# Four instead of three of eight k pairs in the 7-product form, in the three double gate groups of a hybrid attention block

## The chip, the cores and the metric

The kernel runs on one core of a Trainium2 chip. A core has TensorE (PE: matrix products into PSUM), VectorE (DVE: elementwise work on two tensors), ScalarE (ACT: copies, casts and functions), GpSimd (POOL) and SyncE (SP), which issues most DMAs. Each engine works through its own queue in order and waits on semaphores for the others. The metric is the device time of one execution in microseconds (us), as the median of several runs; the kernel before takes 1462.29 us.

## The reference: what is computed

One layer of a residual block over 256 tokens of width 2048, in fp32:

```python
h    = rmsnorm(x, g_mix)
proj = h @ w_in                       # 2048 x 10240: q,k,v | q,k,v | gate_sb | gate_ca
y_sb = stick_breaking_attention(q_sb, k_sb, v_sb)      # 8 heads of 128
y_ca = chunked_relpos_attention(q_ca, k_ca, v_ca, rel_bias)
merged = sigmoid(gate_sb) * (y_sb @ w_sb_out) + sigmoid(gate_ca) * (y_ca @ w_ca_out)
x = x + merged @ w_mix_out
g_ff, u_ff = split(rmsnorm(x, g_ffn) @ w_ffn_in)
x = x + (silu(g_ff) * u_ff) @ w_ffn_out
x = x + sigmoid(rmsnorm(x, g_ple) @ w_ple_gate) * (p @ w_ple_in)
out = rmsnorm(x, g_final)
```

The change lies in the product that gives the two gates, gate_sb and gate_ca: h (256 x 2048) by 2048 x 2048 each.

## The kernel before, in words

**Precision.** Every operand is held as a high part (a cast to fp32r) and a low part (what the cast left). A product of a weight tile with an activation tile is three matmuls: high by high, high by low, low by high (`three`, lines 274 to 277). Weights are streamed from HBM as fp32 tiles of 128 x 1024 (two k tiles of 128 by 512 columns) called `raw`, 512 KB each; ScalarE casts the high part `hi` (line 246, `split`), VectorE subtracts to get the low part `lo` (`minus`, line 228).

**Plain pairs.** The contraction over 2048 runs over 16 k tiles, taken as eight pairs (0 to 7). A double group (`unit`, lines 164 to 183) makes two column blocks of 512 at once, for both token tiles of 128. Per k pair this is a 2 x 2 by 2 x 2 block product: eight products of three matmuls, 24 matmuls. A plain pair comes as two halves, one for each column block, with one `raw`, one `hi` and one `lo` each, and 12 matmuls each.

**Pairs in the 7-product form.** Pairs 2, 4 and 6 (`PAIRS`) are made as seven products of sums and differences, in the manner of Strassen and Winograd: 21 matmuls. For that, `split_pair` (lines 251 to 271) takes both column blocks at once. VectorE makes four differences 512 wide (three into the tile `xf`, one in place in `raw`); ScalarE casts the two raw tiles (lines 261 and 264) and then `xf` (1536 wide, line 267); VectorE makes the three low parts. The 1536-wide parts go into `room`, one place for all pairs of a group, so it is written again only when the pair before has been multiplied. The activations' sums are made ahead in a table, one form per pair: `pair_sums` (line 808 and following) with VectorE and one cast of ScalarE, through a work tile. The forms of the gate groups are in `F_gate`: two in the tile `FP`, one at the end of `room`.

**Sums.** Four of the seven products go to PSUM sums of their own (`su`), kept over all pairs of a group; three go straight into the sums of the plain products (`mm`). After a group's last pair, `mid` (line 817 and following) copies the first sum (ScalarE, line 821) and adds the others (VectorE, line 823, four adds). After the last plain pair `add_sums` (line 827) adds the plain sums, two adds per column block.

**The stage.** The gates' first 512 columns are two ordinary row groups. Then come three double groups, c = 1, 2, 3, each over both gates' columns c, from about 361 us to 486 us of the profile. The last attention steps of the chunked mixer run between these groups as `tasks`; `flush(4)` lets one task go every fourth piece, and the first pair of a double group lets all remaining ones go (`pair_products`, line 288). The value tiles (`v`, tag "v", two places in the pool `mid`) hold the values of attention; the `work` tile takes the place of the last but one of them.

**What sets the order.** `flush` walks through the list of pieces: `prefetch` loads raw tiles while at most five are held, and splits up to three pieces ahead, as long as the pieces from the current one on need at most four `hi`/`lo` buffers; then the piece's products are issued. From this program order a scheduler with its own timeline puts each engine's instructions into a fixed order before the run: where an engine would stand idle it takes a later one that is ready.

The pieces of a double group, "-" for a pair in the 7-product form: 0, 0, 1, 1, -2, 3, 3, -4, 5, 5, -6, 7, 7. The code around the change:

Of the kernel before, what the change touches and what calls it, by code (L numbers as in the profile page):

```python
# [10 lines left out]
F32R = mybir.dt.float32r  # L11
# [5 lines left out]
P = 128  # L17
S = 256
NT = 2
D = 2048  # L20
KD = D // P
HEADS = 8
W = HEADS * P
# [8 lines left out]
NB = 512  # L32
# [2 lines left out]

PAIRS = (2, 4, 6)
MIX_PAIRS = (4, 6)
RAW = 5
MORE = 2
X_LOADS = (3, 5, 6, 7)  # L40
# [3 lines left out]
def block_kernel(ctx: ExitStack, tc: tile.TileContext, x, p, w_in, w_sb_out, w_ca_out, w_mix_out,  # L44
# [43 lines left out]
    T1 = bp.tile([P, KD, 2, S], F32R, tag="T1", name="T1")  # L88
# [51 lines left out]
    pieces = []  # L140
    tasks = deque()
# [19 lines left out]
                needs=[k for k in (needs(kt) for kt in part) if k is not None],  # L161
            ))

    def unit(wsrc, n0s, kts, lhs, forms, ext, slots, mid, post, needs, row0=0, pairs=PAIRS, alone=False, after=None):


        if not alone:
            state["unit"] = state.get("unit", -1) + 1
        pool = 0 if alone else state["unit"] % 2
        g = dict(kind="unit", post=post, mid=mid, slots=slots, after=after, lhs=lhs, keep=None, forms=forms, ext=ext, pool=pool,  # L170
                 side=None if alone else 1 - pool)
        kts = list(kts)
        taken = [j for j in pairs if j < len(kts) // 2 - 1]
        for i in range(len(kts) // 2):
            part = kts[2 * i : 2 * i + 2]
            r = (row0 + 2 * i) * P
            src = [wsrc[r : r + 2 * P, n0 : n0 + NB].rearrange("(k p) n -> p k n", p=P) for n0 in n0s]
            pc = dict(g=g, kts=part, ncol=NB, needs=[needs(kt) for kt in part])
            if i in taken:
                pieces.append(dict(pc, src=src, pair=True, first=i == taken[0], last=i == taken[-1]))  # L180
            else:
                for b in range(2):
                    pieces.append(dict(pc, src=[src[b]], block=b, first=i == 0, last=2 * i + 2 == len(kts)))

    def load_x(c):
        cs = slice(c * NB, (c + 1) * NB)
# [2 lines left out]
    def load_piece(src, ncol):  # L189
        state["ring"] += 1  # L190
        if state["more"] is not None and state["ring"] % (RAW + MORE) in (0, RAW // 2 + 1):
            raw = state["more"]()
        else:
            raw = wp.tile([P, 1024], F32, tag="raw", name="raw", bufs=RAW)
        n = src.shape[1] * ncol
        return raw[:, :n], raw[:, :n].rearrange("p (k n) -> p k n", n=ncol)

    def load(pc):
        at = state["loaded"]
        pc["raw"] = []  # L200
        for src in pc["src"]:
            raw, dst = load_piece(src, pc["ncol"])
            pc["raw"].append(raw)
            state["raw"] += 1
            if at == 0:
                for k in range(2):
                    dma_w.dma_start(dst[:, k, :], src[:, k, :])
                continue
            if at in X_LOADS:
                with tc.issue_after(state["load"].ins):  # L210
                    load_x(X_LOADS.index(at))
            state["load"] = dma_w.dma_start(dst, src)
# [154 lines left out]
    def prefetch():  # L367
        while state["loaded"] < len(pieces) and state["raw"] + len(pieces[state["loaded"]]["src"]) <= RAW + (MORE if state["more"] is not None else 0):
            load(pieces[state["loaded"]])
            state["loaded"] += 1  # L370
        room = 2 if state["at"] < 4 + KD // 2 else 4 if state["fourth"] is not None else 3
        while state["split"] < state["loaded"] and state["split"] <= state["at"] + 3:
            pc = pieces[state["split"]]
            if state["split"] > state["at"] and sum(map(size, pieces[state["at"] : state["split"] + 1])) > room:
                break
            behind = [started["p"]]
            if pc["g"] is pieces[4]["g"]:
                behind += started.get(pc["kts"][0] - 2, [])
            with ExitStack() as order:
                for i in behind:  # L380
                    order.enter_context(tc.issue_after(i.ins))
                split(pc)
            state["split"] += 1

    def later(fn, n=3):

        for _ in range(n):
            tasks.append((None, lambda: None))
        tasks.append((None, fn))
# [76 lines left out]
    mp = mid_stack.enter_context(tc.tile_pool(name="mid", bufs=2))  # L466
# [75 lines left out]
    w2 = w_in[0]  # L542
    hneed = lambda kt: ("hmix", kt)

    def v_tile():
        return mp.tile([P, NT, NB], F32, tag="v", name="v")
# [55 lines left out]
    ext = ap.tile([P, HEADS, 384], F32, tag="gates", name="ext", bufs=1)  # L602
# [162 lines left out]
    def scale_table(T, kts):  # L765

        ks = slice(kts[0], kts[-1] + 1)
        by = p2bc.unsqueeze(1).to_broadcast((P, len(kts), S))
        for c in range(2):
            v = T[:, ks, c, :]  # L770
            nc.vector.tensor_tensor(v, v.bitcast(F32), by, ALU.mult)

    for mixer, make in ((0, sb_tasks), (1, ca_tasks)):
        for b in range(2):
# [3 lines left out]
            first = mixer == 0 and b == 0  # L778
            v = v0 if first else v_tile()
# [9 lines left out]
            if end:  # L789
                group("row", w2, c0 + 2 * W, range(KD), T1, lambda ps, v=v: scale_v(v, ps), needs=hneed,  # L790
                      after=lambda kts: scale_table(T1, kts))
# [9 lines left out]
    room = bp.tile([P, 4096], F32R, tag="x", name="room")  # L801
# [4 lines left out]
    F_gate = [FP[:, 0], FP[:, 1], room[:, 3072:].rearrange("p (c f s) -> p c f s", c=2, f=4)]  # L806

    def pair_sums(T, kt, f):
        af = state["work"]("af").rearrange("p (k s) -> p k s", k=2)
        hi, lo = (T.bitcast(F32)[:, kt : kt + 2, c, :] for c in range(2))  # L810
        nc.vector.tensor_tensor(af, hi, lo, ALU.add)
        sums_of(af, f)

    def gate_slots(c):
        return [gates[:, t, m, c * NB : (c + 1) * NB] for m in range(2) for t in range(NT)]
# [13 lines left out]
    for m in range(2):  # L829
        group("row", w2, 6 * W + m * D, range(KD), T1, gate_post(m, 0), needs=hneed)  # L830
    flush(3)
    for i, pair in enumerate(PAIRS):
        pair_sums(T1, 2 * pair, F_gate[i])
    for c in range(1, 4):
        unit(w2, [6 * W + m * D + c * NB for m in range(2)], range(KD), T1, lambda kt: F_gate[kt // 4 - 1],
             [room[:, :3072]], lambda c=c: gate_slots(c), mid, add_sums, hneed, alone=True)
    flush(4)
    state["fourth"] = None
    x_ = bp.tile([P, NT, D], F32, tag="x", name="x")
# [3 lines left out]
    def out_post(m, c):  # L843
        def post(ps):
# [6 lines left out]
            if m == 1:  # L851
                mg = gates[:, :, 0, cs]
                nc.vector.tensor_tensor(mg, mg, gt, ALU.add)
                later(lambda: into_table(T1, c, mg, key="mg", forms=lambda kt: FP[:, kt // 4 - 2], pairs=MIX_PAIRS))
        return post

    for c in range(4):
        for m, wo in ((0, w_sb_out), (1, w_ca_out)):
            group("row", wo[0], c * NB, range(8 * m, 8 * m + 8), T2, out_post(m, c),
                  needs=lambda kt: ("y", kt))  # L860
# [60 lines left out]
    for c in (0, 2):  # L921
        unit(w_mix_out[0], (c * NB, (c + 1) * NB), range(KD), T1, lambda kt: FP[:, kt // 4 - 2], mix_rooms, C_slots,
             mid, mix_post(c), lambda kt: ("mg", kt), pairs=MIX_PAIRS)
    flush(until=("mg", KD - 1))
# [73 lines left out]
    for blk, nk in enumerate(FF_BLOCKS):  # L998
        key = f"h{blk}"
        for c in range(nk // 4):  # L1000
            j = k0 // 4 + c
            unit(w_ffn_in[0], (j * NB, D_FF + j * NB), range(KD), T3, lambda kt: late["F"][0][kt // 4 - 1], rooms(T1),
                 C_slots, mid, (in_post if j else first_post)(T2, c, key), lambda kt: ("ffn", kt),
                 pairs=PAIRS if j else (), after=None if j else scale_next)
        last = blk == len(FF_BLOCKS) - 1
# [122 lines left out]
```

## Time and profile before

| what | value |
|---|---|
| median of 3 runs | 1462.29 us (1461.79 to 1462.46) |
| the profiled execution's own time (its span) | 1460.0 us |
| instructions | 18637 |
| bytes moved by DMA | 291.19 MB, mean 199 GB/s |
| granted TensorE clock, mean | 0.999 |

In the page, a row of the groups reads: line of the kernel, engine, operation, output tile <- input tiles, shapes, count; then the busy time in us, the mean of one in ns, and the idle time of the engine just before such instructions with what ended it. In a timeline a row is: start in us, duration, engine, line, operation, tiles, shapes, count, and in brackets the engine's idle time just before and who ended it. Durations of neighbouring instructions overlap, since they are pipelined: what one more of them costs is read from start to start. In a table of stretches each engine has its busy time in us and its count of instructions; PEld is TensorE's weight load. The idle time of an engine that is not the bottleneck costs nothing.

### The profile page before, as it was taken

What the parts mean: (1) busy time and instruction counts of PE and PEld (TensorE: products, weight loads), DVE (VectorE), ACT (ScalarE), POOL (GpSimd) and SP (SyncE); (2) the same over time, 40 slices, a digit from 0 to 9 for tenths busy, and PEclk for the clock granted to TensorE, in tenths of its full rate; (3) what the DMA queues carried; (4) which work ended last, traced back from release to release, by engine and by line L of the source; (5) the groups of instructions that cost most, each with busy time, mean ns of one, the idle gap of its engine ahead of it and who ended that gap; (6) DMA issues with size and microseconds to landing.
All of it is one profiled execution on the core that took longest, in us unless ns stands there. A gap on an engine that the chain in (4) does not pass through costs nothing.

```text
span 1460.0 us, 18637 instructions
## 1 busy us (share of the span) xinstructions
PE 1449.5 (99%) x6867; PEld 1213.5 (83%) x6867; DVE 1209.2 (83%) x1524; ACT 800.4 (55%) x950; POOL 21.9 (1%) x44
## 2 busy tenths in 40 slices
PE   9999999999999999999999999999999999999997
PEld 7888888888888888888888888888888888888886
DVE  6666667796888667988999999999999989989775
ACT  6455555557555444555555555565645555556552
POOL 0100000000000000000000000000000000000000
PEclk9999999999999999999999999999999999999999
DMA  9855555565666766766666666666666666666772
GB/s 320 283 176 174 173 173 180 179 190 161 212 196 207 236 188 188 238 191 180 194 189 200 189 208 208 202 195 210 194 195 202 203 193 195 216 199 209 229 228 73
DMA packets 164733, 291.19 MB, mean 199 GB/s; under 512 B 9025, under 2 KB 42097, under 8 KB 164385
## 3 DMA queue, kind: packets, MB, share of 16 engines
q1 hardware_dynamic: 162528, 281.32, 61.9%
q0 software_dynamic: 2112, 8.68, 1.8%
q8 instruction: 54, 0.88, 0.2%
q14 instruction: 39, 0.31, 0.1%
HBM read 284.19 MB, written 5.77 MB: 199 GB/s over the span
## 4 chain that ended last, share of the span: by engine, by line
PE 99%; DMA 0%; DVE 0%; ACT 0%; SPq 0%; issue 0%; DVEq 0%
PE mm L276 24%; PE mm L277 24%; PE mm L275 24%; PE mm L351 8%; PE mm L353 4%; PE su L275 4%; PE su L276 4%; PE su L277 4%; PE tp L434 1%; DMA raw<-in_w_ple_in 0%; PE yp L659 0%; PE xps L488 0%; PE wt L750 0%; PE mml L277 0%; PE mml L276 0%; PE mml L275 0%
## 5 line engine op out<-in xcount | busy, mean ns | idle before, releaser
L228 DVE TENSOR_TENSOR lo<-raw,hi 128x1024 fp32r<-128x1024 f32 (+1 forms) x517 | 627.5, 1220 | 168.4 <-ACT hi L246 158.6
L246 ACT CAST hi<-raw 128x1024 fp32r<-128x1024 f32 (+1 forms) x399 | 418.1, 1051 | 427.9 <-PE mm L277 316.2
L276 PE MATMUL mm<-lo,T 128*128 128x512 f32 x1391 | 542.4, 390 | 0.0
L277 PE MATMUL mm<-hi,T 128*128 128x512 f32 x1391 | 538.9, 390 | 0.0
L275 PE MATMUL mm<-hi,T 128*128 128x512 f32 x1391 | 512.6, 391 | 0.0
L277 PEld LDWEIGHTS mm<-hi,T 128*128 128x128 f32 x1391 | 261.1, 188 | 53.8
L276 PEld LDWEIGHTS mm<-lo,T 128*128 128x128 f32 x1391 | 261.2, 188 | 53.4
L275 PEld LDWEIGHTS mm<-hi,T 128*128 128x128 f32 x1391 | 260.9, 188 | 53.6
L351 PE MATMUL mm<-T,hi 128*128 128x512 f32 x512 | 180.7, 399 | 0.0
L353 PE MATMUL mm<-T,lo 128*128 128x256 f32 x512 | 140.8, 280 | 0.0
L351 PEld LDWEIGHTS mm<-T,hi 128*128 128x128 f32 x512 | 95.4, 188 | 21.5
L264 ACT CAST hi<-raw 128x1024 fp32r<-128x1024 f32 x59 | 62.3, 1055 | 70.5 <-DVE raw L228 20.0
L353 PEld LDWEIGHTS mm<-T,lo 128*128 128x128 f32 x512 | 96.4, 189 | 1.2
L228 DVE TENSOR_TENSOR T<-xf,T 128x1536 fp32r<-128x1536 f32 x50 | 87.8, 1755 | 7.9 <-ACT T L267 7.9
L228 DVE TENSOR_TENSOR xf<-raw 128x512 f32<-128x512 f32 x118 | 80.9, 686 | 9.5 <-DMA raw<-in_w_in 4.9
L267 ACT CAST T<-xf 128x1536 fp32r<-128x1536 f32 x50 | 74.0, 1480 | 7.9 <-DVE xf L228 7.8
L261 ACT CAST hi<-raw 128x1024 fp32r<-128x1024 f32 x59 | 62.2, 1054 | 28.9 <-PE mm L277 22.8
L823 DVE TENSOR_TENSOR C<-su,C 128x512 f32<-128x512 f32 x72 | 47.7, 684 | 0.2
L827 DVE TENSOR_TENSOR C<-mm,C 128x512 f32<-128x512 f32 x72 | 46.9, 683 | 0.0
L228 DVE TENSOR_TENSOR xf<-raw,xf 128x512 f32<-128x512 f32 x59 | 40.4, 685 | 0.3
L228 DVE TENSOR_TENSOR raw<-raw 128x512 f32<-128x512 f32 x59 | 40.4, 685 | 0.1
L277 PE MATMUL mm<-T,T 128*128 128x512 f32 (+1 forms) x82 | 30.2, 368 | 0.0
(310 smaller groups left out, 1369.1 us busy)
## 6 DMA issues: line engine op xcount, KB each, us to landing
raw<-in_w_ffn_in SPq DMA_DIRECT2D x176, 512.0 KB, 3.9
raw<-in_w_in SPq DMA_DIRECT2D x160, 512.0 KB, 3.6
raw<-in_w_ffn_out SPq DMA_DIRECT2D x88, 512.0 KB, 4.6
raw<-in_w_mix_out SPq DMA_DIRECT2D x32, 512.0 KB, 4.7
raw<-in_w_ple_gate SPq DMA_DIRECT2D x32, 512.0 KB, 4.8
raw<-in_w_sb_out SPq DMA_DIRECT2D x16, 512.0 KB, 4.6
raw<-in_w_ca_out SPq DMA_DIRECT2D x16, 512.0 KB, 4.6
x<-in_x SPq DMA_DIRECT2D x4, 512.0 KB, 10.3
```

Source lines behind the costliest of these rows:

```text
L228: return nc.vector.tensor_tensor(out, a, b, ALU.subtract)
L246: state["cast"] = nc.scalar.copy(hi[:, c : c + m], raw[:, c : c + m])
L261: nc.scalar.copy(h1, raw1)
L264: nc.scalar.copy(h2, raw2)
L267: nc.scalar.copy(xh, xf)
L275: nc.tensor.matmul(ps, xh, hi, start=a, stop=False)
L276: nc.tensor.matmul(ps, xh, lo, start=False, stop=False)
L277: state["mm"] = nc.tensor.matmul(ps, xl, hi, start=False, stop=z)
L351: nc.tensor.matmul(ps, hi[:, i, f], lhs[:, kt, :, :].rearrange("p c s -> p (c s)"), start=a, stop=False)
L353: nc.tensor.matmul(ps[:, :S], lo[:, i, f], lhs[:, kt, 0, :], start=False, stop=z)
L823: nc.vector.tensor_tensor(C[i], q, C[j], ALU.add)
L827: nc.vector.tensor_tensor(g["C"][i], g["ps"][i], g["C"][i], ALU.add)
```

## The change

The three double gate groups take pairs 1, 3, 5 and 6 in the 7-product form instead of 2, 4 and 6. The pieces of a group come in an order written out by hand; between pairs 1 and 3, and between 5 and 6, stands one half of a plain pair, between 3 and 5 stand two halves of different pairs:

0, 0, -1, 2, -3, 2, 4, -5, 4, -6, 7, 7

`unit` takes this list as `order`; a pair's first mention is its first column block, the second its second. Without a list it builds the same order as before, so that the other double groups (mix and feed-forward) keep theirs. Three forms are made where the three were made, for the new pairs. The fourth is made in a task that comes last in the list of tasks, in a tile that takes a place of the value tiles (tag "v"), which is free once attention has used the last values.

```diff
+GATE_PAIRS = (1, 3, 5, 6)
+GATE_ORDER = (0, 0, -1, 2, -3, 2, 4, -5, 4, -6, 7, 7)
...
-    def unit(wsrc, n0s, kts, lhs, forms, ext, slots, mid, post, needs, row0=0, pairs=PAIRS, alone=False, after=None):
+    def unit(wsrc, n0s, kts, lhs, forms, ext, slots, mid, post, needs, row0=0, pairs=PAIRS, alone=False, after=None,
+             order=None):
...
-        taken = [j for j in pairs if j < len(kts) // 2 - 1]
-        for i in range(len(kts) // 2):
+        if order is None:
+            order = [j for i in range(len(kts) // 2) for j in ([-i] if i in pairs and i < len(kts) // 2 - 1 else [i, i])]
+        taken = [-i for i in order if i < 0]
+        begun = set()
+        for i in order:
+            own = i < 0
+            i = abs(i)
...
-            if i in taken:
+            if own:
                 pieces.append(dict(pc, src=src, pair=True, first=i == taken[0], last=i == taken[-1]))
             else:
-                for b in range(2):
-                    pieces.append(dict(pc, src=[src[b]], block=b, first=i == 0, last=2 * i + 2 == len(kts)))
+                b = int(i in begun)
+                begun.add(i)
+                pieces.append(dict(pc, src=[src[b]], block=b, first=i == 0, last=2 * i + 2 == len(kts)))
...
-    for i, pair in enumerate(PAIRS):
+    for i, pair in enumerate(GATE_PAIRS[:3]):
         pair_sums(T1, 2 * pair, F_gate[i])
+
+    def last_form():
+        F_gate.append(mp.tile([P, 2, 4, P], F32R, tag="v", name="F_v"))
+        pair_sums(T1, 2 * GATE_PAIRS[3], F_gate[3])
+
+    tasks.append((None, last_form))
     for c in range(1, 4):
-        unit(w2, [6 * W + m * D + c * NB for m in range(2)], range(KD), T1, lambda kt: F_gate[kt // 4 - 1],
-             [room[:, :3072]], lambda c=c: gate_slots(c), mid, add_sums, hneed, alone=True)
+        unit(w2, [6 * W + m * D + c * NB for m in range(2)], range(KD), T1, lambda kt: F_gate[GATE_PAIRS.index(kt // 2)],
+             [room[:, :3072]], lambda c=c: gate_slots(c), mid, add_sums, hneed, alone=True, order=GATE_ORDER)
```

## The prediction

> **What bounds the kernel now.** I read the page first (busy shares and groups), then the stretch table for the three double groups, then the timelines of VectorE, ScalarE and TensorE inside the third of them.
>
> ```profile
> span 1460.0 us, 18637 instructions
> PE 1449.5 (99%) x6867; PEld 1213.5 (83%) x6867; DVE 1209.2 (83%) x1524; ACT 800.4 (55%) x950; POOL 21.9 (1%) x44
> L276 PE MATMUL mm<-lo,T 128*128 128x512 f32 x1391 | 542.4, 390 | 0.0
> ```
>
> TensorE is never released late: the last column of its groups, idle time, is 0.0. A busy 99% alone would not prove this, because matmuls overlap; their starts do.
>
> ```profile
> 463.53 0.39 PE L275 MATMUL su<-hi,T 128*128 128x512 f32 x1
> 463.75 0.39 PE L276 MATMUL su<-lo,T 128*128 128x512 f32 x1
> 463.98 0.39 PE L277 MATMUL su<-hi,T 128*128 128x512 f32 x1
> 466.25 0.39 PE L275 MATMUL su<-room,FP 128*128 128x512 f32 x1
> 466.93 0.39 PE L276 MATMUL su<-room,FP 128*128 128x512 f32 x1
> ```
>
> One matmul takes 0.39 us, but the next starts 0.22 or 0.23 us later. So a matmul that is saved is worth its step, not its 390 ns. The step comes from one period of the double groups. The copy of the first sum (line 821) marks it:
>
> ```profile
> 393.69 0.59 ACT L821 COPY gates<-su 128x512 f32<-128x512 f32 x1 [0.30 <-PE su L277]
> 435.17 0.59 ACT L821 COPY gates<-su 128x512 f32<-128x512 f32 x1 [0.26 <-PE su L277]
> 476.64 0.59 ACT L821 COPY gates<-su 128x512 f32<-128x512 f32 x1 [0.26 <-PE su L277]
> ```
>
> ```profile
> core 0: us, PE busy (x) PEld busy (x) DVE busy (x) ACT busy (x) POOL busy (x), PEclk, DMA share, GB/s
> 393.69:435.17 41.48, 41.48 (x184) 34.35 (x183) 36.04 (x40) 24.05 (x25) 0.00 (x0) 1.00 0.66 202
> 435.17:476.64 41.47, 41.47 (x184) 34.35 (x183) 36.08 (x40) 23.96 (x24) 0.00 (x0) 1.00 0.65 202
> ```
>
> A group has three pairs of 21 matmuls and five plain pairs of 24, together 183, as the weight loads (x183) show. 41.47 / 183 = 0.2266 us a step, at a granted clock of 1.00. TensorE bounds this stage. VectorE is next: 36.08 us busy, so 5.39 us idle in a group. ScalarE has 17.5 us idle, and the DMA engines work 0.65 of the time.
>
> **What the change takes away.** A fourth pair in each of three groups goes from 24 matmuls to 21: 3 x 3 x 0.2266 = 2.04 us. A group becomes 180 x 0.2266 = 40.79 us. This is all it can bring, since nothing else on TensorE goes.
>
> **What it adds on VectorE and ScalarE.** The pair form needs four 512-wide differences and a 1536-wide low part on VectorE, and a 1536-wide cast on ScalarE. The two 1024-wide casts and low parts are there in both forms. This is the last pair of the third group now:
>
> ```profile
> 464.62 0.68 DVE L228 TENSOR_TENSOR xf<-raw 128x512 f32<-128x512 f32 x1
> 465.22 1.22 DVE L228 TENSOR_TENSOR lo<-raw,hi 128x1024 fp32r<-128x1024 f32 x1
> 466.36 0.68 DVE L228 TENSOR_TENSOR raw<-raw 128x512 f32<-128x512 f32 x1
> 466.96 1.22 DVE L228 TENSOR_TENSOR lo<-raw,hi 128x1024 fp32r<-128x1024 f32 x1
> 468.09 0.68 DVE L228 TENSOR_TENSOR xf<-raw 128x512 f32<-128x512 f32 x1
> 468.70 1.22 DVE L228 TENSOR_TENSOR lo<-raw,hi 128x1024 fp32r<-128x1024 f32 x1
> 469.83 0.68 DVE L228 TENSOR_TENSOR xf<-raw,xf 128x512 f32<-128x512 f32 x1
> 472.14 1.76 DVE L228 TENSOR_TENSOR room<-xf,room 128x1536 fp32r<-128x1536 f32 x1 [1.62 <-ACT room L267]
> 473.81 3.83 DVE L228 TENSOR_TENSOR lo<-raw,hi 128x1024 fp32r<-128x1024 f32 x3
> ```
>
> Start to start a difference takes 0.60 us, a 1024-wide low part 1.13, the 1536-wide one 1.67. The new pair adds 4 x 0.60 + 1.67 = 4.07 us, and VectorE's work becomes 36.08 + 4.07 = 40.15 us in a group of 40.79. Its idle time has to shrink from 5.39 to 0.64 us, or it becomes the bound. ScalarE's extra cast (1.48 us, row below) fits into its 17.5 us.
>
> **The fourth form (last_form).** It is made once, from three kinds of rows like these:
>
> ```profile
> 324.87 0.69 DVE L811 TENSOR_TENSOR work<-T 128x512 f32<-128x512 f32 x1
> 328.46 0.28 DVE L418 TENSOR_TENSOR work<-work 128x128 f32<-128x128 f32 x1
> 328.66 0.49 DVE L228 TENSOR_TENSOR work<-work 128x128 f32<-128x128 f32 x2
> 333.12 0.69 DVE L228 TENSOR_TENSOR room<-work,room 128x512 fp32r<-128x512 f32 x1
> ```
>
> ```profile
> L659 PE MATMUL yp<-a,v x8: 270/272/274, 336.0 to 364.5; 128*128 128x128 f32 x8
> ```
>
> Two of 0.60 and four of about 0.20 us (start to start) give 2.0 us of VectorE, in the first group. Its tile is free once the last values are used, at 364.5 us; the form is needed by the group's fourth pair, after the plain halves and three pairs, some 25 us later. So its wait costs nothing, only its time counts. The other three forms move to other pairs at the same price and are done before 334 us (the row at 333.12), well ahead of the groups. Weight loads: the same 16 transfers of 512 KB per group in another order, on the same queue; SP and POOL are passed by nothing new.
>
> **The closer order.** Pairs -1 and -3, and -5 and -6, now have one plain half between them instead of two. From pair to pair TensorE takes 33 steps, 7.48 us; VectorE needs a pair (4.07 + 2 x 1.13 = 6.33) and a half (1.13), 7.46 us. So there is no slack inside these two places, and it must be caught up elsewhere. One room holds the 1536-wide operands: its cast can start only when the earlier pair has ended.
>
> ```profile
> 470.63 1.48 ACT L267 CAST room<-xf 128x1536 fp32r<-128x1536 f32 x1 [2.37 <-DVE xf L228]
> 461.81 1.76 DVE L228 TENSOR_TENSOR room<-xf,room 128x1536 fp32r<-128x1536 f32 x1 [1.62 <-ACT room L267]
> ```
>
> Cast and low part take 1.48 + 0.03 + 1.76, about 3.4 us with the hand-over. By the written order the low part is read 13 matmuls into the next pair, so a half and 13 steps, 25 x 0.2266 = 5.7 us, lie between. That fits by 2.3 us, unless other VectorE work stands ahead. Behind a late low part in VectorE's queue stand the low parts of the next plain halves, which TensorE reads next.
>
> **The sum.** Over three groups VectorE has 3 x 0.64 = 1.9 us to spare and the form takes 2.0: 0.1 us over, if it never waited. How much must it wait when it is this full? The trace does not show this order; the nearest are the fullest stretches of the later stages, where TensorE also ran without a gap:
>
> ```profile
> 680.00:720.00 40.00, 40.00 (x182) 33.13 (x181) 38.95 (x59) 21.44 (x24) 0.00 (x0) 1.00 0.63 184
> 920.00:960.00 40.00, 40.00 (x182) 33.16 (x181) 38.76 (x49) 23.67 (x26) 0.00 (x0) 1.00 0.65 198
> ```
>
> There VectorE idles 1.05 and 1.24 us in 40. Over 122.4 us this makes 3.2 to 3.8 us. Against it stands the lead: in the third group the low part ends at 463.57 and would be read, by the written order, at 463.53 + 13 x 0.2266 = 466.48, 2.9 us later. This lead is used up once. TensorE so stands still for 0.1 + (3.2 to 3.8) - 2.9 = 0.4 to 1.0 us. I take 0.8, near the upper end, because these stretches have table work to fill waits which the gate groups lack. The lower bound is 0 (no gap), the upper one is the third case below. 2.04 - 0.8 = 1.24 us are kept. The profiled execution's 1460.0 us becomes 1458.8; the median of the runs, 1462.29, lies 2.29 us above that execution's span, which the change does not touch: **1461.0 us**.
>
> **The rivals.**
>
> *All of it is kept.* VectorE's idle time now is only time in which it has no work, and the planner fills it. For: where it is loaded most, it ran adds, differences and low parts from 937.29 to 945.7 us in twelve instructions without a wait:
>
> ```profile
> 937.29 0.68 DVE L827 TENSOR_TENSOR C<-mm,C 128x512 f32<-128x512 f32 x1
> ...
> 944.48 1.22 DVE L228 TENSOR_TENSOR lo<-raw,hi 128x1024 fp32r<-128x1024 f32 x1
> ```
>
> Against: 0.64 us of idle time in a group is less than any 40 us of the trace show. It gives 1462.29 - 2.04 = 1460.25 us. Chance 0.32; the forecast 0.45.
>
> *VectorE becomes the bound: slower.* Its wait for the 1536-wide cast, 1.62 us in two of three pairs now, stays unfilled at two of the four pairs, -1 and -5. There the next half cannot yet be cast, since four buffers of high and low parts are all held, and VectorE has nothing to put in between. A group then takes 40.15 + 2 x 1.62 = 43.39 us; three make 130.2, with the form 2.0 more, less the lead 2.9: 129.3 against 124.4 now, +4.9 us, 1467.2 us. It decides once VectorE waits over 0.64 us in a group and the lead is used up; slower by 2.9 us needs 2.04 + 2.9 us given back, that is 4.9 + 2.9 - 0.1 = 7.7 us of waits, 2.6 in a group. For: those waits in the rows above. Against: they appear where VectorE runs ahead; when it falls behind, TensorE has released the buffers and the next half is ready to fill them. Chance 0.17.
>
> *VectorE already rules.* The occupancy it has now, 36.08 of 41.47 us (87%), is all it gets through with these waits. Then a group takes 40.15 / 0.87 = 46.1 us, three 13.9 us more: 1476.2 us. Against: two stretches above hold 97%. Chance 0.04. The Trainium skill, Perfetto Trace Analysis, "Identifying the Most-Contended Engine", speaks for it: the engine with the highest occupancy is to be relieved first, and TensorE is to be judged by its weight loads, not by its matmuls. By that rule VectorE (36.08) stands ahead of the weight loads (34.35) and the change loads the wrong engine; the trace does not agree as yet, since TensorE starts a matmul every 0.2266 us with no gap.
>
> That the change does not do what it says I give 0.02, and any time near the old one: the order names each plain pair twice and each of 1, 3, 5, 6 once, 180 matmuls.
>
> **How the numbers follow.** 0.2% of this kernel, 2.9 us, is about what a measurement can tell from no change. No case is faster by that much, since 2.04 us is all there is: 0.02 for what I have not seen. Slower by over it are the rule case and most of the second rival: 0.16. The rest, 0.82, lies within. The range goes from 1459.9 (all kept, with the spread of the runs, about 0.35 us) up to 1465.2, 2.9 us above the kernel now: beyond it lie only the slower cases' 0.16, below it a few hundredths.
>
> **What would show it.** Right: 180 weight loads from one copy at line 821 to the next, a period of 40.8 to 41.2 us, VectorE busy 40 us of it, small gaps in TensorE's starts at pairs -3 or -6. All kept: 40.8 and no gap. Wrong: a period over 42.4 us, with waits of 1.6 us before the 1536-wide low part and TensorE waiting for `room` or `lo`; or losses outside the 361 to 486 us that hold the three groups; or TensorE waiting for `raw`, which I rule out on the DMA share of 0.65.

## The result

| kernel | median (from, to), us | ratio to before, 95% interval | span of the profiled execution, us |
|---|---|---|---|
| before | 1461.81 (1461.70 to 1462.46) | | 1460.0 |
| after | 1468.54 (1467.74 to 1469.98) | 1.0045 [1.0034, 1.0056] | 1468.2 |

The changed kernel is slower by 6.7 us; 1461.0 was forecast, at most 1465.2. Of its runs the profiled one was the longest, so its span is 8.2 us above that of before.

### The profile page after: what moved, and what is told of

Its sections match the earlier page's. It is cut to its first block, busy times and chain, and to the rows that moved or that the text cites. A ratio compares the mean times of both kernels' runs of the same rounds, so it can differ in the third digit from the quotient of the medians.

```text
span 1468.2 us, 18639 instructions
## 1 busy us (share of the span) xinstructions
PE 1451.3 (99%) x6858; PEld 1212.9 (83%) x6858; DVE 1224.1 (83%) x1545; ACT 803.8 (55%) x954; POOL 21.9 (1%) x44
## 4 chain that ended last, share of the span: by engine, by line
PE 97%; DVE 1%; DMA 1%; ACT 0%; issue 0%; SPq 0%; DVEq 0%; ACTq 0%
PE mm L285 23%; PE mm L286 23%; PE mm L284 23%; PE mm L360 8%; PE mm L362 4%; PE su L285 4%; PE su L286 4%; PE su L284 4%; PE tp L443 1%; DMA raw<-in_w_ple_in 1%; DVE lo L237 1%; DMA raw<-in_w_in 0%; DVE gates L832 0%; PE yp L668 0%; PE xps L497 0%; DVE xf L237 0%
## 5 line engine op out<-in xcount | busy, mean ns | idle before, releaser
L255 ACT CAST hi<-raw 128x1024 fp32r<-128x1024 f32 (+1 forms) x393 | 411.4, 1050 | 419.3 <-PE mm L286 310.8
L285 PE MATMUL mm<-lo,T 128*128 128x512 f32 x1370 | 534.5, 390 | 0.0
L286 PE MATMUL mm<-hi,T 128*128 128x512 f32 x1370 | 531.1, 390 | 0.0
L284 PE MATMUL mm<-hi,T 128*128 128x512 f32 x1370 | 506.5, 391 | 2.6 <-DVE gates L836 2.6
L284 PEld LDWEIGHTS mm<-hi,T 128*128 128x128 f32 x1370 | 257.0, 188 | 56.6 <-DVE gates L836 3.9
L286 PEld LDWEIGHTS mm<-hi,T 128*128 128x128 f32 x1370 | 257.3, 188 | 53.2
L285 PEld LDWEIGHTS mm<-lo,T 128*128 128x128 f32 x1370 | 257.4, 188 | 52.5
L273 ACT CAST hi<-raw 128x1024 fp32r<-128x1024 f32 x62 | 65.3, 1054 | 74.5 <-DVE raw L237 30.8
L237 DVE TENSOR_TENSOR xf<-raw 128x512 f32<-128x512 f32 x124 | 85.1, 686 | 8.0 <-DMA raw<-in_w_in 2.8
L270 ACT CAST hi<-raw 128x1024 fp32r<-128x1024 f32 x62 | 65.3, 1053 | 32.5 <-PE mm L286 22.9
L285 PE MATMUL su<-lo,T 128*128 128x512 f32 x74 | 29.4, 398 | 2.8 <-DVE lo L237 2.8
```

The costliest lines, as they stand in the source:

```text
L237: return nc.vector.tensor_tensor(out, a, b, ALU.subtract)
L255: state["cast"] = nc.scalar.copy(hi[:, c : c + m], raw[:, c : c + m])
L270: nc.scalar.copy(h1, raw1)
L273: nc.scalar.copy(h2, raw2)
L284: nc.tensor.matmul(ps, xh, hi, start=a, stop=False)
L285: nc.tensor.matmul(ps, xh, lo, start=False, stop=False)
```

## The profile after

The page first: the span, the busy shares, and the two groups of TensorE's matmuls with idle time in the last column.

```profile
span 1468.2 us, 18639 instructions
PE 1451.3 (99%) x6858; PEld 1212.9 (83%) x6858; DVE 1224.1 (83%) x1545; ACT 803.8 (55%) x954; POOL 21.9 (1%) x44
L284 PE MATMUL mm<-hi,T 128*128 128x512 f32 x1370 | 506.5, 391 | 2.6 <-DVE gates L836 2.6
L285 PE MATMUL su<-lo,T 128*128 128x512 f32 x74 | 29.4, 398 | 2.8 <-DVE lo L237 2.8
```

The busy shares are those of before, 99 and 83 per cent. What is new is idle time on TensorE, where before had 0.0. The stretch table, from one copy of a first sum to the next (now line 830), shows how much:

```profile
core 0: us, PE busy (x) PEld busy (x) DVE busy (x) ACT busy (x) POOL busy (x), PEclk, DMA share, GB/s
393.74:438.98 45.24, 43.05 (x187) 34.75 (x186) 40.48 (x46) 24.86 (x26) 0.00 (x0) 1.00 0.59 186
438.98:485.78 46.80, 42.70 (x181) 34.62 (x180) 40.07 (x46) 24.99 (x25) 0.00 (x0) 0.96 0.56 178
```

VectorE works 40.5 and 40.1 us in a period, as the sum had it (40.15). But the period is 45.2 and 46.8 us instead of 40.8 to 41.2, so VectorE *idles* 4.8 and 6.7 us where it was to idle 0.64. (The copies do not stand at the same place of each group's order, hence 186 and 180 loads.) In the second period the granted clock is 0.96.

The starts of neighbouring matmuls say where TensorE stood. Every start that comes more than one step of 0.2267 us behind the one before counts as a pause by what it is late. Between 366 and 500 us the pauses add up to 9.90 us, against 0.13 before. With 2.04 us saved, and 0.46 more in the first 20 us, that makes +8.2 us, the whole difference of the two spans. None lies at the second, third or fourth pair of a group: all are where one group ends and the next begins, up to that group's first pair. The waits of TensorE between 20 and 1440 us (in total, times, longest; before has none):

```profile
PE su L285 <- DVE lo L237: 2.8, 2, 2.6
PE mm L284 <- DVE gates L836: 2.6, 3, 1.5
PE su L284 <- ACT room L276: 1.2, 1, 1.2
```

TensorE's timeline at the second of the two boundaries:

```profile
444.44 0.39 PE L286 MATMUL mm<-hi,T 128*128 128x512 f32 x1
446.37 0.50 PE L284 MATMUL mm<-hi,T 128*128 128x512 f32 x1 [1.53 <-DVE gates L836]
...
448.08 0.39 PE L284 MATMUL mm<-hi,T 128*128 128x512 f32 x1
451.03 0.80 PE L285 MATMUL su<-lo,T 128*128 128x512 f32 x1 [2.56 <-DVE lo L237]
451.63 0.63 PE L286 MATMUL su<-hi,T 128*128 128x512 f32 x1
452.05 0.63 PE L285 MATMUL mm<-lo,T 128*128 128x512 f32 x1
...
454.07 0.40 PE L284 MATMUL su<-room,FP 128*128 128x512 f32 x1
```

First the new group's first plain matmul waits for a PSUM bank that `add_sums` (line 836) must empty; then its first pair waits for a low part. The next seven steps, 451.03 to 454.07, take 3.04 us instead of 7 x 0.2267 = 1.59: another 1.4 us, and no engine is waited for. VectorE's timeline of the same microseconds:

```profile
443.22 0.69 DVE L237 TENSOR_TENSOR xf<-raw 128x512 f32<-128x512 f32 x1 [1.41 <-DMA raw<-in_w_in]
443.83 0.68 DVE L832 TENSOR_TENSOR gates<-su,gates 128x512 f32<-128x512 f32 x1
444.43 0.68 DVE L237 TENSOR_TENSOR raw<-raw 128x512 f32<-128x512 f32 x1
445.03 0.68 DVE L832 TENSOR_TENSOR gates<-su,gates 128x512 f32<-128x512 f32 x1
445.63 0.68 DVE L836 TENSOR_TENSOR gates<-mm,gates 128x512 f32<-128x512 f32 x1
446.23 0.68 DVE L237 TENSOR_TENSOR xf<-raw 128x512 f32<-128x512 f32 x1
446.83 1.28 DVE L832 TENSOR_TENSOR gates<-su,gates 128x512 f32<-128x512 f32 x2
448.03 1.22 DVE L237 TENSOR_TENSOR lo<-raw,hi 128x1024 fp32r<-128x1024 f32 x1
```

And before, at its first boundary:

```profile
395.12 0.69 DVE L823 TENSOR_TENSOR gates<-su,gates 128x512 f32<-128x512 f32 x1 [0.47 <-PE su L277]
395.72 1.22 DVE L228 TENSOR_TENSOR lo<-raw,hi 128x1024 fp32r<-128x1024 f32 x1
396.86 2.01 DVE L823 TENSOR_TENSOR gates<-su,gates 128x512 f32<-128x512 f32 x3
398.78 0.68 DVE L827 TENSOR_TENSOR gates<-mm,gates 128x512 f32<-128x512 f32 x1
399.38 0.68 DVE L228 TENSOR_TENSOR xf<-raw 128x512 f32<-128x512 f32 x1
```

Before, the group's four sum adds and the first `mm` add come first, then the next group's first difference. After, three differences of the next group's first pair stand ahead of the adds or between them, in a fixed order, and the first waits 1.41 us for its weight tile, with the adds queued behind it. TensorE's order has changed as well. This is the first boundary after the change:

```profile
397.40 0.39 PE L284 MATMUL su<-room,F_v 128*128 128x512 f32 x1
...
399.21 0.39 PE L286 MATMUL mm<-room,T 128*128 128x512 f32 x1
...
400.57 0.39 PE L286 MATMUL mm<-hi,T 128*128 128x512 f32 x1
401.73 0.50 PE L284 MATMUL mm<-hi,T 128*128 128x512 f32 x1 [0.77 <-DVE gates L836]
```

The last pair's 1536-wide products, which complete the four sums, are followed by only six matmuls of the group: 18 of the last plain pair's 24 were put ahead of them. Before, all 24 come behind them. So VectorE's adds begin late, and TensorE needs the banks at 400.80, 1.6 us after the first of eight begins:

```profile
399.18 0.69 DVE L832 TENSOR_TENSOR gates<-su,gates 128x512 f32<-128x512 f32 x1 [0.29 <-PE su L286]
```

**Theories.** *Order*: the two fixed orders make the adds late; with better orders nearly all comes back. *Close pairs*: four pairs do not fit because `room` and the half between two pairs are too tight (the prediction's slower rival). *Width*: after a last pair come four halves before the next first pair, six before the change, so VectorE's work there no longer fits. *Load*: VectorE simply has too much to do. *Form*: `last_form` and its 2.0 us.

## The experiments

"Pauses" are the sum of TensorE's pauses from 366 to 500 us, made as above (0.13 before, 9.90 after). They belong to the one profiled execution, not to the median. Ratios are to the kernel before, on the same chip. What an edit "gives back" is the distance of its median from 1468.54 us. Edits are against the changed kernel.

**Three pairs in an early order, and four pairs begun later.**

```diff
+GATE_PAIRS = (1, 4, 6)
+GATE_ORDER = (0, 0, -1, 2, 2, 3, 3, -4, 5, 5, -6, 7, 7)
...
-    tasks.append((None, last_form))
```

```diff
+GATE_PAIRS = (2, 3, 5, 6)
+GATE_ORDER = (0, 0, 1, -2, 1, -3, 4, -5, 4, -6, 7, 7)
```

> Three pairs again (1, 4 and 6), so VectorE has no more work than in the kernel before (36.1 us in a group) and no fourth form; but the first pair stands right behind the two first halves, as in the changed kernel: four halves between a group's last pair and the next group's first, where the kernel before has six. Theory A (collision at the group boundary: the eight end adds and the first pair's VectorE work fall together there): both boundaries lose as in the changed kernel, 3 to 6 us each, so 1466 to 1471 us. Theory B (VectorE is too full in sum, wherever the pairs stand): no loss, 1461.8 us within 1. Theory C (TensorE's fixed order puts the last pair's 1536-wide products behind the last plain halves, so the end adds begin late): no number of its own, the loss follows that order.

> Four pairs as in the change, but 2, 3, 5 and 6 in the order 0 0 1 -2 1 -3 4 -5 4 -6 7 7: five halves over the boundary instead of four, and one half in each of the three places inside. VectorE's work is that of the changed kernel. Theory A: each boundary has 2.7 us more of TensorE as cover, the losses of 2.8 and 5.8 us shrink to about 0 and 2, and 2.04 us are saved: 1460 to 1463 us. Theory B: as the changed kernel, 1467 to 1470 us.

Three early: 1464.37 us, 1.0017 [1.0008, 1.0026], pauses 3.25, all at the two boundaries. So even three pairs lose when the first one comes early. VectorE's timeline of it shows the same pattern as after: a difference waits for its weight tile, the adds stand behind.

```profile
394.80 0.69 DVE L237 TENSOR_TENSOR xf<-raw 128x512 f32<-128x512 f32 x1 [1.73 <-DMA raw<-in_w_in]
...
397.15 0.68 DVE L832 TENSOR_TENSOR gates<-su,gates 128x512 f32<-128x512 f32 x1
```

Four later: 1465.99, 1.0028 [1.0018, 1.0038], pauses 6.07, the greatest of them (2.31 us at 400.38) again at a boundary, with `su` waiting for the adds of line 832. Beginning later gives back over a third of the 6.7 us.

**The adds first on VectorE.** The first pair's first two differences are queued behind the four sum adds of the group before.

```diff
+        with ExitStack() as behind:
+            if pc["first"] and pc["g"]["side"] is None and "adds" in state:
+                behind.enter_context(tc.issue_after(state["adds"].ins))
...
-            nc.vector.tensor_tensor(C[i], q, C[j], ALU.add)
+            state["adds"] = nc.vector.tensor_tensor(C[i], q, C[j], ALU.add)
```

> The changed kernel, with the first pair's two first differences on VectorE queued behind the last of the four adds on the former group's product sums; in the changed kernel they stand ahead of and between these adds, and one waits 1.4 us for its raw tile. Theory D (this order and the wait for the raw tile make the loss): 1463 to 1466 us. Theory A (too much VectorE work for four halves, in any order): the adds come earlier but the pair later, 1467 to 1470 us.

1463.23, 1.0008 [0.9999, 1.0017], pauses 3.83. This one rule gives back 5.3 of the 6.7 us. All waits of TensorE that are left are short:

```profile
PE mm L287 <- DVE gates L839: 1.4, 5, 0.3
```

TensorE's order at the end of a group is the old one, with six matmuls behind the last pair. VectorE's timeline at the first boundary now shows what that costs: it idles until the late products of the last pair are done.

```profile
399.09 1.42 DVE L835 TENSOR_TENSOR gates<-su,gates 128x512 f32<-128x512 f32 x2 [2.30 <-PE su L289]
```

The edge did not move VectorE's instructions alone. The scheduler answered it on TensorE as well: at the first boundary, the first pair's first matmul with a low part is the 27th behind the last pair's products instead of the 16th. The gain is that of the edge with what the scheduler made of it.

**The same rule with three early pairs.**

```diff
+GATE_PAIRS = (1, 4, 6)
+GATE_ORDER = (0, 0, -1, 2, 2, 3, 3, -4, 5, 5, -6, 7, 7)
...
+                behind.enter_context(tc.issue_after(state["adds"].ins))
```

> e1_three_early (three pairs, the first one right behind the first halves) with the end adds ahead of the next first pair's differences. Theory D (the order of the adds on VectorE is what the early first pair costs): e1's 2.4 us go, 1461.8 us within 0.7. Theory A (the work over four halves is too much in any order): 1463.5 to 1464.5 us, as e1.

1462.16, 1.0000 [0.9991, 1.0010], pauses 0.25, no wait of TensorE left. For three pairs the order is the whole loss, since VectorE's work is the same. Here TensorE has all 24 matmuls of the last plain pair behind the last pair with and without the edge, and the first matmul with a low part moves only from the 34th to the 39th.

**TensorE's last pair in turn.** Pair 7's plain matmuls must come behind the last pair's products; then the same with the adds first.

```diff
+            state.setdefault("seven", deque(maxlen=7)).append(state["mm"])
...
+                if pc["last"] and g["side"] is None:
+                    for i in state["seven"]:
+                        turn.enter_context(tc.issue_after(i.ins))
```

> The changed kernel, with TensorE's matmuls of the last plain pair (7) of a gate group queued behind all seven products of the group's last pair. Theory C: the end adds begin up to 1.4 us earlier at the first boundary and so at the second, most of the loss goes: 1461 to 1465 us. Theories A and B: the work on VectorE is the same, so 1467 to 1470 us, or worse, since TensorE then waits where it filled its time with plain products.

> e3_pe_in_turn and e4_adds_first together: the last plain pair's matmuls stand behind the last pair's products, and the end adds ahead of the next pair's differences. Theory C2: the sums end 2.7 us or more earlier, the adds are done before the next group needs their banks, and what is left is the wait for the 1536-wide part, which e3 shows as 0.3 to 2.2 us a group: 1462 to 1465 us. Theory A: 1463 to 1464 us, as e4. Above 1466 us the order of TensorE's matmuls alone is worth more than the adds' order.

1467.86, 1.0038 [1.0024, 1.0052], pauses 8.24; with the adds first 1467.78, 1.0039 [1.0024, 1.0054], pauses 9.26. Both expectations of a gain failed. TensorE is now made to stand before the 1536-wide low part, which is late when only the last pair is held in turn:

```profile
478.76 0.39 PE L284 MATMUL mm<-room,T 128*128 128x512 f32 x1
481.37 0.50 PE L285 MATMUL su<-room,F_v 128*128 128x512 f32 x1 [2.22 <-DVE room L237]
```

**Every pair in turn.** All plain matmuls of the gate groups stay behind the pair before them, so that each pair releases `room` early, not only the last; with and without the adds first.

```diff
-                if pc["last"] and g["side"] is None:
-                    for i in state["seven"]:
+                if g["side"] is None:
+                    for i in state.get("seven", ()):
```

> As e13_all_turn_adds, but with the order of VectorE left to the planner as in the changed kernel. Theory D alone decides: 1464 to 1468 us; theory E alone: 1461 us within 1.

> e4_adds_first with all plain matmuls of the gate groups queued behind the pair before them on TensorE, so that each pair's 1536-wide products keep their place, the room comes free earlier and the end adds start with six steps of TensorE more in front of the boundary. Theory E: pauses of 3.8 us in e4 fall below 1.5: 1460.3 to 1461.7 us, faster than both kernels. Theory B: TensorE waits inside the groups for VectorE's 1536-wide parts instead, as in e3 and e7 (1.5 to 2.4 us at a time): 1463 to 1467 us.

In turn alone: 1462.85, 1.0006 [0.9997, 1.0015], pauses 3.00. With the adds first: 1463.78, 1.0011 [1.0002, 1.0020], pauses 4.15. So an edge on TensorE alone, with VectorE's order left to the scheduler, gives back 5.7 us; the two remedies do not add up. In turn alone, the differences still stand among the sum adds, but the first add now comes ahead of them and 4.3 us earlier than in the changed kernel (394.91 against 399.18 us):

```profile
394.91 0.69 DVE L837 TENSOR_TENSOR gates<-su,gates 128x512 f32<-128x512 f32 x1 [0.18 <-PE su L286]
...
396.65 0.68 DVE L237 TENSOR_TENSOR xf<-raw 128x512 f32<-128x512 f32 x1
```

No wait for a PSUM bank is left at the boundaries. The waits are short ones for the 1536-wide low part, 0.5 us at the first pair of the second and third groups and 0.2 at their second, the only one of the two where the prediction had looked:

```profile
PE su L285 <- DVE room L237: 1.4, 4, 0.5
```

**A second place for the 1536-wide parts** (with the adds first, then with every pair in turn). Six 512-wide tiles that attention has left serve every second pair.

```diff
+        parts = [ap.tile([P, NB], F32R, tag=u, name="more", **({} if u == "bias" else dict(bufs=1)))
+                 for u in ("sh", "sl", "e", "ls", "bias", "bias")]
+        gate_rooms[0] = (parts[:3], parts[3:])
```

> e4_adds_first with a second place for the 1536-wide parts, in tiles that attention has left (their cast and low part there are three of 512 each, some 0.3 us more per pair). Theory E (the single room is a chain: a pair's cast waits for the last product of the pair before, so the fourth pair's 1536-wide products come last of the group, the end adds late): the first group's last pair comes in time, e4's 1.3 us of pauses after the first group go, and the 1.5 us after the second as far as the planner's order follows: 1461 to 1462.5 us. Theory B (VectorE is full in sum): 1463 us or more, since VectorE has more to do.

> e13_all_turn with the second place for the 1536-wide parts of e12. Of e13's 3.0 us of pauses, 2.0 are at the first and 0.7 to 1.0 at the second pair of the second and third groups, where TensorE waits for the 1536-wide low part. Theory E (the single place makes these waits): they go, 1460.3 to 1461.3 us. Theory A and B (VectorE has 15.7 us of work over a boundary of 15.6 and 40.2 in a group of 40.8): the first pair's wait stays, 1462.3 to 1463.5 us.

1462.53, 1.0006 [0.9997, 1.0014], pauses 4.19: the first boundary's pauses are gone (0.01 us between 395 and 412 us, where the adds first have 1.18), the others stay short, and one new pause lies behind the groups:

```profile
489.71 0.73 PE L299 MATMUL mm<-hi,T 128*128 128x512 f32 x2 [1.40 <-ACT hi L255]
```

The cast that TensorE waits for there had itself waited for a weight tile to land (ScalarE idle 7.93 us at 488.61), so this pause need not be in the other runs. With every pair in turn 1463.56, 1.0011 [1.0002, 1.0020], pauses 3.57. So the single `room` takes a part in the late order, but a second one does not bring the saving out.

**Another order of the pairs, `room` used last** (with the adds first).

```diff
+GATE_PAIRS = (1, 3, 4, 6)
+GATE_ORDER = (0, 0, -1, 2, -3, 2, -4, 5, 5, -6, 7, 7)
...
+                behind.enter_context(tc.issue_after(state["adds"].ins))
```

> As e4_adds_first (four pairs, the end adds ahead of the next first pair's differences), but the two halves between pairs stand ahead of the last pair: 0 0 -1 2 -3 2 -4 5 5 -6 7 7, so that the last pair's 1536-wide parts have a half more time. Theory C2 (what is left in e4 comes from the last pair: its 1536-wide parts are late behind one half only, TensorE fills with the last plain halves, the end adds start late): the waits of 0.45 us at the boundaries go, 1460.5 to 1462 us. Theory A (too much VectorE work over four halves): as e4, 1463 us within 0.7.

1466.33, 1.0029 [1.0018, 1.0041], pauses 6.66, many of 0.3 to 0.5 us, some inside the groups. The order on record is the better one.

**Wider boundaries.** Group 2 with three pairs, so that six and five halves lie over the two boundaries; then with the adds first, then with every pair in turn.

```diff
+GATE_ORDER = {1: (0, 0, -1, 2, -3, 2, 4, -5, 4, -6, 7, 7),
+              2: (0, 0, 1, 1, -3, 2, 2, -5, 4, 4, -6, 7, 7),
+              3: (0, 0, 2, -1, 2, -3, 4, -5, 4, -6, 7, 7)}
```

> Four pairs in the first and the third gate group only, the second with three (3, 5 and 6, with 0 0 1 1 ahead), the third with its first pair behind five halves: over the boundaries stand six and five halves instead of four and four. The order of the adds is left to the planner. It can save 2 x 3 x 0.2266 = 1.36 us. Theory A (the width of the boundary decides): no pause at either boundary, 1460.7 us within 0.5. Theory D (the first pair's differences ahead of the end adds decide): the planner puts them so again at five halves, 1463 to 1466 us, as in e2.

> As e9_mixed, with the end adds ahead of the next first pair's differences. Theories A and D together: 1460.7 us within 0.5, which would be faster than both kernels. If VectorE's sum inside the groups with four pairs costs of itself (theory B), each of them keeps the 1 us that e4 has left over per group: 1461.8 to 1463 us.

> e13_all_turn with e9's orders: four pairs in the first and third group, three in the second, six and five halves over the boundaries. 1.36 us can be saved. Theory A and B: VectorE has slack again at both boundaries, pauses under 0.6 us in all: 1460.7 to 1461.5 us. If the pauses come from the two pairs with one half between them in the third group, 0.3 to 0.7 us are lost there: 1461.2 to 1461.8 us.

1465.14, 1.0021 [1.0012, 1.0030]; 1463.87, 1.0011 [1.0003, 1.0020]; 1463.02, 1.0006 [0.9998, 1.0015]. The second of them has six halves behind group 1 and still pauses there (1.09 us at 400.04, 1.21 at 402.85), and none behind group 2, which has three pairs. So *width* falls as the main cause: a group of four pairs ends late itself. Of the rest it takes a part. The third has no pause at the wide boundary behind group 1, where in turn alone the next first pair paused 0.86 us, and nearly all of its pauses lie in its four-pair third group (2.18 of 2.45 us):

```profile
PE su L287 <- DVE room L239: 1.2, 2, 0.7
```

**Less work on VectorE: two of sixteen low parts per group on GpSimd** (with the adds first).

```diff
+            if pc["g"]["kind"] == "unit" and pc["g"]["side"] is None and pc["block"] == 0 and (pc["first"] or pc["last"]):
+                low = lambda *t: nc.gpsimd.tensor_tensor(*t, ALU.subtract)
```

> As e4_adds_first, with two of the 16 low parts of a group (the first halves of pairs 0 and 7, next to the boundary) made by GpSimd instead of VectorE; this takes 2.3 us of VectorE's 40 in a group, all at the boundary. Theory A (VectorE work at the boundary is the price): 1460.3 to 1462 us. Rival: GpSimd takes so long for 128 x 1024 (its time is not in any trace here; the bound is that a half must be there within the 5 us before it is read) or slows VectorE so that TensorE waits for it: 1463 us or more.

1467.47, 1.0038 [1.0023, 1.0053], pauses 7.94: worse than the adds first alone, so it does not test *load* cleanly. GpSimd's groups and VectorE's timeline say why (two of GpSimd's six subtracts begin at 389.19 and 393.02 us):

```profile
L258 POOL TENSOR_TENSOR lo<-raw,hi 128x1024 fp32r<-128x1024 f32 x6 | 18.1, 3030 | 182.5 <-ACT hi L255 113.1 <-DVE lo L237 69.4
```

```profile
388.31 1.22 DVE L237 TENSOR_TENSOR lo<-raw,hi 128x1024 fp32r<-128x1024 f32 x1
390.09 2.79 DVE L237 TENSOR_TENSOR lo<-raw,hi 128x1024 fp32r<-128x1024 f32 x1 [0.56 <-ACT hi L255]
...
394.48 3.40 DVE L237 TENSOR_TENSOR lo<-raw,hi 128x1024 fp32r<-128x1024 f32 x1
```

**No fourth form.** The fourth pair takes the third pair's.

```diff
-        F_gate.append(mp.tile([P, 2, 4, P], F32R, tag="v", name="F_v"))
-        pair_sums(T1, 2 * GATE_PAIRS[3], F_gate[3])
+        F_gate.append(F_gate[2])
```

> The changed kernel without the fourth form: the fourth pair multiplies with the third pair's form (the values of that pair's products are then not the reference's). VectorE has 2.0 us less and ScalarE 0.6 less, once, in the first group. If the form eats VectorE's lead, the first boundary's 2.8 us go and the second follows: 1464 to 1467 us. If it was made in idle time, no change: 1468.5 us within 1.

1468.84, 1.0046 [1.0032, 1.0060], pauses 9.69 at the same places. The form costs nothing that can be measured.

## Why the prediction was wrong

**The step that failed** is in the sum: "There VectorE idles 1.05 and 1.24 us in 40. Over 122.4 us this makes 3.2 to 3.8 us." It took the idle time of other stages for that of the gate groups, and set a lead of 2.9 us against it. VectorE idled 11.5 us in two periods alone, and TensorE's standstill, 0.8 us in the sum, measured 9.8. (Part of this idle time may follow from the pauses themselves: ScalarE's cast at 453.19 us, behind the longest of them, waited 0.85 us for TensorE to release its buffer.) The groups of VectorE from 361 to 486 us after the change show in their last column what ended its idle time:

```profile
L237 DVE TENSOR_TENSOR lo<-raw,hi 128x1024 fp32r<-128x1024 f32 x47 | 56.7, 1220 | 5.5 <-ACT hi L255 3.0 <-ACT hi L270 2.2
L237 DVE TENSOR_TENSOR room<-xf,room 128x1536 fp32r<-128x1536 f32 x11 | 19.3, 1755 | 6.4 <-ACT room L276 6.4
L237 DVE TENSOR_TENSOR xf<-raw 128x512 f32<-128x512 f32 x22 | 15.1, 688 | 2.2 <-DMA raw<-in_w_in 2.0
```

An engine of fixed order with 40.15 us of work for 40.79 has 0.64 us to spare for an operand that is late, and it met three kinds, up to 1.6 us late.

**The place.** The prediction made its closest account for the pairs with one half between them (7.46 of 7.48 us) and looked for gaps there. The ledger was never drawn over the boundary: four low parts, eight adds and a pair, 4 x 1.13 + 8 x 0.60 + 6.33 = 15.7 us of VectorE, against 69 steps of TensorE, 15.6 us. Before, with six halves, it was 17.9 against 21.1 us. This ledger shows where to look; that it is not the cause alone, the wide boundary that still paused with the adds first showed.

**"SP and POOL are passed by nothing new"** was said of queues, and VectorE's own was left out. The early first pair brought its differences among the end adds, and this is shown as a cause: the adds first give back 5.3 us with four pairs, with TensorE's late last pair as it was, and 2.2 of 2.4 us with three. The other order, TensorE's, is shown too: in turn alone gives back 5.7 us, with differences still among the adds. Either unties most of the knot. How much of each gain comes from the other instructions that the scheduler moved with the edge is not shown.

**The waits for `raw`**, ruled out on a mean DMA share of 0.65: TensorE never waited for `raw`, but VectorE did, 1.41 us, with the adds behind it. A mean share says nothing on when one tile lands. But such a wait is not new, and it need not cost anything. This one is in the kernel before, inside the first group, where TensorE has no pause:

```profile
381.57 0.69 DVE L228 TENSOR_TENSOR xf<-raw 128x512 f32<-128x512 f32 x1 [2.36 <-DMA raw<-in_w_in]
```

Nor does the loss need it. With wider boundaries alone, VectorE has no wait for `raw` at the first boundary (it had waited 1.80 us for a cast of ScalarE at 397.95). The differences stand among the adds as in the changed kernel, and TensorE pauses 2.34 and 1.14 us there for the adds:

```profile
399.25 0.69 DVE L239 TENSOR_TENSOR xf<-raw 128x512 f32<-128x512 f32 x1
399.86 0.68 DVE L834 TENSOR_TENSOR gates<-su,gates 128x512 f32<-128x512 f32 x1
```

What the wait adds in the changed kernel was not tried by itself.

**"The form takes 2.0"**: 0 that can be measured, since TensorE does not pause in the first group with it or without it. Its work was priced rightly and its effect on the time was not.

**The slower rival** (1467.2, chance 0.17) was nearest in size, by a mechanism that was not the one: VectorE waited 6.4 us for the 1536-wide cast, less than before the change, where the same group reads:

```profile
L228 DVE TENSOR_TENSOR room<-xf,room 128x1536 fp32r<-128x1536 f32 x9 | 15.8, 1756 | 7.6 <-ACT room L267 7.6
```

TensorE waited for `room` once, 1.16 us at pair -1 of the second group, and there the cast was late because its differences stood among the adds. Only with the orders mended do pauses of 0.3 to 0.9 us at `room` come to the front, most of them at a group's first pair.

**The rule rival** (1476.2): the Trainium skill, Perfetto Trace Analysis, "Identifying the Most-Contended Engine", would by its weight-load measure relieve VectorE first. (The section names a second measure for TensorE, MFU, its share of the peak matmul rate, which the prediction left out.) It was right in sign, +6.7 us for its 13.9, though VectorE was never full: with 40 us of work it did not fill its 45 us.

**Right** were the 180 loads (2.04 us saved), VectorE's 40.1 us, ScalarE's room for the cast, and that cast and low part fit between two close pairs: no pause lies there, not even the small gaps at -3 or -6 that were to show the forecast right.

**Open.** With either order mended, 2.5 to 4.2 us of mostly short pauses eat the 2.04 saved (1.36 in the wider boundaries). A second `room` and wider boundaries, each also with the order in turn, did not remove them; how much is `room` and how much VectorE's load is not settled. No version ran faster than the kernel before.

## What to carry to other kernels

Before adding work to an engine that has a little idle time, draw its ledger over the narrowest stretch between two things that TensorE needs, group boundaries above all, and not over the mean period. Then ask which of the added instructions the scheduler may put ahead of one that frees a buffer or a PSUM bank: in a fixed order, an early instruction holds everything behind it, the more so when it waits for a transfer. An ordering edge, which adds no work, can tell such a cause from a lack of throughput in one run; compare the orders of all engines afterwards, since the scheduler may move more than the edge names.

## What the runs showed of the hardware

**Half speed after a pause.** In the stretch after the 2.56-us wait the granted clock was 0.53 (the third column from the end):

```profile
451.00:454.10 3.10, 3.07 (x8) 2.45 (x9) 3.10 (x4) 2.04 (x3) 0.00 (x0) 0.53 0.85 264
454.10:458.00 3.90, 3.90 (x19) 3.23 (x18) 3.13 (x4) 2.43 (x4) 0.00 (x0) 1.00 0.37 113
```

Seven or eight matmuls 0.427 us apart came after pauses of 2.72 us (the kernel after, and again without the fourth form), 2.31 (four later), 2.38 (last pair in turn, 1.5 us after TensorE had resumed), 1.72 (GpSimd) and 1.67 and 1.51 (last pair in turn and adds first). Each stretch lasted 3.0 to 3.4 us at a granted clock of 0.51 to 0.56, and 1.4 to 1.6 us were lost each time. They did not come after 2.34 (wider boundaries), 1.70 (the kernel after) and 1.56 (second `room`). So pauses of 1.5 to 2.7 us were followed by 1.4 us more in some cases and not in others, and their length alone does not decide. These steps are in the pauses above: 1.6 us of the 8.24 with the last pair in turn, 3.1 of the 9.26 with the adds first besides. Versions that differ by so little are not to be ranked by their pauses. The Trainium skill, TensorE: Matmul & The Clock Gate, "Part 1: The HAM clock gate", gives half rate after at least one idle window of about 3.4 us, a window that runs freely. The rate of about half agrees (0.427 against 0.2267 us a step); the pauses here were all shorter than that.

**GpSimd beside VectorE.** A subtract of 128x1024 took GpSimd 3.03 us on average, and VectorE's own beside it 2.79 and 3.40 instead of 1.22 us. From 361 to 486 us VectorE's differences and low parts together took 108.8 us, with five low parts fewer, against 105.9 in the adds first: moving the low parts cost VectorE more than it saved.
